# One raw weight tile fewer, one pair of split weight tiles more, in a two-block transformer kernel on one core

## The chip, the core and the metric

One NeuronCore of a Trainium2 chip runs the whole program. The metric is device microseconds (us) of one execution; three executions of the kernel before were timed, and a fourth was profiled.

## The reference, cut to what matters

A sequence of 512 tokens of width 1024 goes through two blocks. The first has two layers, each with three kinds of attention (MLA, differential, chunked) and a gated feed-forward part with a short convolution; the second has a forgetting attention, a state-space part and a mixture of 32 experts. Nearly all of its arithmetic is products with weight matrices:

```python
proj = rms_norm(x, attn_norm[l]) @ w_in[l]
...
x = x + jnp.concatenate([o_mla, o_diff, o_ch], axis=-1) @ w_out[l]
x = x + conv_ffn(rms_norm(x, ffn_norm[l]), w_ffn_in[l], ffn_conv_w[l], ffn_conv_b[l], w_ffn_out[l])
...
z = h @ w_in[l]
mixed = (jax.nn.sigmoid(g_attn) * (y_attn @ w_proj_attn[l])
         + jax.nn.sigmoid(g_ssm) * (y_ssm @ w_proj_ssm[l]))
```

## The kernel before, in words

Each product is computed in three TensorE passes over parts in a reduced format (fp32r): a weight tile `w` is split into `wh` (its rounded value) and `wl` (the rest), the input is split in the same way, and `mm3` (L300 to L304) adds hi by hi, hi by lo and lo by hi. So a weight tile goes through three places:

- `weights` (L306) takes a raw tile `w` of up to 128 x 1024 f32 (4 KB a partition) from pool `wfp` and has SyncE (SP) issue its load from HBM (L311);
- `split` (L291) has ScalarE (ACT) write `wh` (L294) and VectorE (DVE) write `wl` (L295), in a pair of 4 KB tiles from pool `wsp`;
- `proj` (L317) has TensorE (PE) multiply from the pair, 128 columns at a time (L302 to L304).

Before, `wfp` has three raw tiles and `wsp` two pairs. A pair is free again when PE has done its last multiplication from it; a raw tile is free when DVE has written its `wl`. The tiles of the attention inputs (`wp`, `wu`), of the output projections (`wo1` with 640 columns, `wo2` with 768), of the feed-forward parts (`wfi`, `wfo`), and of the second block's `wz`, `wglu`, `wps`, `wpa` (the last three with 512 columns) and `wo` all pass through these two pools. The experts' weights do not: they have pools of their own (`raw`, `mh`, `ml`, L1953 and L1956).

The order of the instructions is set by a planner of the tile framework when the program is built: it plays the program through with estimated durations and gives each engine, at each moment, the ready instruction of highest priority (the order of the program text, with lifts by `prior` for the softmax, L574, and the normalization helpers). An instruction whose tile has no free buffer is not ready. On the chip, each engine, and SP's queue too, then runs that fixed order, waiting on semaphores. From the last step of the second block's output projection on (the experts), the order is that of the program text (L1625).

`newton` (L343) computes a reciprocal square root on DVE in a dozen tiny instructions; its temporaries `nyi` and `na` had six buffers of 32 bytes each (the default of pool `smp`).

The stages, by time in the profile: the first layer's attention to about 305 us, its feed-forward part to 668; the second layer's attention to 958, its feed-forward part to 1320; the second block's mixer to about 1730 and its experts to the end.

Of the kernel before, what the change touches and what calls it, by code (L numbers as in the profile page):

```python
# [57 lines left out]
NRAW = (6, 2, 0, 2)  # L58
# [174 lines left out]
    return a  # L233


BUFS = {"vf": 1, "xs": 2, "sqa": 1, "PT": 6, "E": 4, "B": 2, "V": 2, "u": 5, "lp": 1, "sm": 8, "rs": 8, "ss": 8, "od": 1, "ofd": 2, "xh": 2, "xl": 2, "ye": 3, "raw0": NRAW[0], "raw1": NRAW[1], "raw2": NRAW[2], "raw3": NRAW[3], "mh": 5, "ml": 4, "mh2": 2, "ml2": 2, "ind": 1, "xr": 4, "ud": 4, "fd": 1, "xrd": 1, "stab": 1, "sl": 7, "ix": 7, "yb": 1, "ld": 1, "Bd": 1, "hld": 16, "vd": 8, "gad": 1, "ya": 4, "gs": 8, "ga": 3, "wr": 1, "rsel": 1, "wm": 2, "wr2": 2}


def prior(offset):
# [9 lines left out]
class K:  # L249
# [6 lines left out]
    def T(self, pool, shape, dt, tag):  # L256
        self.n += 1
        return pool.tile(shape, dt, tag=tag, name=f"{tag}_{self.n}", bufs=BUFS.get(tag))

# [930 lines left out]
    def wpart(self, tag):  # L1190

        n = self.parts[tag]
        self.parts[tag] += 1
        return self.T(self.mw2, [128, 1024], F32R, tag + "2") if n % (2 + BUFS[tag]) < 2 else self.T(self.mw, [128, 1024], F32R, tag)

# [838 lines left out]
```

## Time and profile before

| | |
|---|---|
| three timed runs | 2059.34, 2064.02, 2066.14 us; median 2064.02 |
| the profiled execution's own time | 2062.34 us |
| its span, first to last instruction | 2060.6 us |
| mean granted TensorE clock | 0.986 of full speed |
| PE, DVE, ACT busy | 97%, 72%, 53% of the span |
| DMA | 343.7 MB moved, 167 GB/s in the mean |

A wait in the profile is idle time of an engine just before an instruction, put down to what released it. "Busy" of PE counts modelled ends of pipelined multiplications, so it is not a measure of speed by itself: a 128x512 multiplication is shown as some 0.39 us long, though the next one starts some 0.23 us after it. PEld is the loading of the stationary operand, which overlaps PE.

### The profile page before, as it was taken

The page shows a single profiled execution, that of the slowest core. Times are in us where ns is not written, and L with a number is a line of the kernel's source. Part 1 is how long each engine was busy: PE and PEld are TensorE (multiplying, and loading weights), DVE is VectorE, ACT ScalarE, POOL GpSimd, SP SyncE. Part 2 cuts the span into 40 slices and gives each one's busy share as a digit, 9 for nine tenths or more (in the row PEclk, how much of TensorE's full clock was granted, in tenths as well). Part 3 has the DMA queues.
Part 4 walks back from the last instruction along what each step waited for, and adds up shares of the span by engine and source line. Part 5 has one row for each costly group of instructions (what it writes and reads, how often), then busy time and mean ns, then how long its engine had stood idle before and what let it go on. Part 6 is the DMA issues. An engine that isn't in the chain of part 4 may idle for free.

```text
span 2060.6 us, 28191 instructions
## 1 busy us (share of the span) xinstructions
PE 1990.3 (97%) x9836; PEld 1603.3 (78%) x9836; DVE 1478.9 (72%) x2763; ACT 1086.7 (53%) x1760; POOL 64.6 (3%) x132
## 2 busy tenths in 40 slices
PE   7998999999999999989999999999999998999997
PEld 6776778888888878767888888788887876778885
DVE  6787887777633577877777744688756576899996
ACT  5475644444423366644444433334358445788886
POOL 0000000000000000000000000000000000111111
PEclk9998999999999999999999999999999999999999
DMA  5565552323344345634323234344346383899994
GB/s 162 153 196 179 179 166 93 98 97 101 100 123 138 124 125 172 182 127 153 103 92 102 93 113 130 119 157 132 118 152 191 123 282 95 323 333 404 393 405 145
DMA packets 133874, 343.74 MB, mean 167 GB/s; under 512 B 29050, under 2 KB 42618, under 8 KB 121058
## 3 DMA queue, kind: packets, MB, share of 16 engines
q1 hardware_dynamic: 128946, 329.08, 47.4%
q0 software_dynamic: 4640, 12.73, 2.5%
q8 instruction: 79, 1.29, 0.3%
q14 instruction: 65, 0.53, 0.1%
q10 hardware_dynamic: 144, 0.10, 0.0%
HBM read 293.18 MB, written 46.96 MB: 165 GB/s over the span
## 4 chain that ended last, share of the span: by engine, by line
PE 82%; DVE 9%; DMA 3%; ACT 3%; issue 2%; SPq 1%; POOL 0%; DVEq 0%; POOLq 0%; ACTq 0%
PE acc L302 21%; PE acc L303 21%; PE acc L304 21%; PE t L536 2%; DVE ml L1956 2%; PE t L608 2%; PE t L362 1%; PE s L304 1%; PE s L302 1%; PE s L303 1%; DVE wl L295 1%; PE o L548 1%; PE s L850 1%; PE o L549 1%; ACT wh L294 1%
## 5 line engine op out<-in xcount | busy, mean ns | idle before, releaser
L302 PE MATMUL acc<-hb,wh 128*128 128x512 f32 x1392 | 550.5, 396 | 17.4 <-ACT hb L297 11.4
L304 PE MATMUL acc<-hb,wl 128*128 128x512 f32 x1392 | 548.3, 394 | 2.9 <-DVE wl L295 2.8
L303 PE MATMUL acc<-hb,wh 128*128 128x512 f32 x1392 | 547.7, 394 | 0.9 <-DVE hb L295 0.7
L294 ACT ACTIVATE wh<-w 128x1024 fp32r<-128x1024 f32 (+3 forms) x263 | 257.1, 977 | 513.4 <-PE acc L303 371.3
L295 DVE TENSOR_TENSOR wl<-w,wh 128x1024 fp32r<-128x1024 f32 (+3 forms) x263 | 294.9, 1122 | 148.4 <-ACT wh L294 147.8
L302 PEld LDWEIGHTS acc<-hb,wh 128*128 128x128 f32 x1392 | 263.0, 189 | 73.3 <-ACT hb L297 11.4
L304 PEld LDWEIGHTS acc<-hb,wl 128*128 128x128 f32 x1392 | 262.3, 189 | 57.4 <-DVE wl L295 5.4
L303 PEld LDWEIGHTS acc<-hb,wh 128*128 128x128 f32 x1392 | 262.5, 189 | 54.2 <-DVE hb L298 1.4
L1956 DVE TENSOR_TENSOR ml<-raw,mh 128x1024 fp32r<-128x1024 f32 x196 | 231.5, 1224 | 5.9 <-ACT mh L1953 5.1
L1953 ACT ACTIVATE mh<-raw 128x1024 fp32r<-128x1024 f32 x196 | 196.9, 1054 | 8.2 <-DMA raw<-in_we 4.3
L304 PE MATMUL acc<-hid,wl 128*128 128x512 f32 x320 | 126.4, 395 | 0.0
L302 PE MATMUL acc<-hid,wh 128*128 128x512 f32 x320 | 126.4, 395 | 0.0
L303 PE MATMUL acc<-hid,wh 128*128 128x512 f32 x320 | 126.3, 395 | 0.0
L302 PE MATMUL acc<-mh,xh 128*128 128x512 f32 x264 | 108.0, 409 | 0.0
L303 PE MATMUL acc<-ml,xh 128*128 128x512 f32 x264 | 104.6, 396 | 0.0
L304 PE MATMUL acc<-mh,xl 128*128 128x512 f32 x264 | 104.6, 396 | 0.0
L941 DVE TENSOR_TENSOR raw<-acc,R 128x512 f32<-128x512 f32 x88 | 60.6, 688 | 60.7 <-PE acc L304 60.2
L592 ACT ACTIVATE E<-E,mx 128x512 f32<-128x512 f32 (+3 forms) x160 | 88.7, 555 | 27.5 <-DVE mx L590 26.4
L295 DVE TENSOR_TENSOR PT<-t,PT 128x512 fp32r<-128x512 f32 (+1 forms) x120 | 69.2, 597 | 19.1 <-ACT PT L294 18.3
L945 ACT ACTIVATE cv<-raw,sp 128x512 f32<-128x512 f32 x88 | 71.8, 816 | 18.1 <-DVE raw L941 18.1
L536 PE MATMUL t<-cst,E 128*128 128x128 f32 x400 | 74.0, 289 | 5.3 <-DVE E L858 2.7
L294 ACT ACTIVATE PT<-t 128x512 fp32r<-128x512 f32 (+1 forms) x120 | 59.9, 526 | 33.7 <-PE t L536 23.1
(545 smaller groups left out, 3271.8 us busy)
## 6 DMA issues: line engine op xcount, KB each, us to landing
raw<-in_we SPq DMA_DIRECT2D x99, 1024.0 KB, 17.8
w<-in_wfi SPq DMA_DIRECT2D x88, 512.0 KB, 3.4
w<-in_wp SPq DMA_DIRECT2D x34, 512.0 KB, 4.0
w<-in_wfo SPq DMA_DIRECT2D x32, 512.0 KB, 3.6
w<-in_wz SPq DMA_DIRECT2D x32, 512.0 KB, 3.8
hld<-tf SPq DMA_DIRECT2D x56, 256.0 KB, 2.3
qk<-hld SPq DMA_DIRECT2D x96, 128.0 KB, 3.7
qk<-hld SPq DMA_DIRECT2D x192, 64.0 KB, 1.9
```

The lines of the kernel that those rows point to most:

```text
L294: nc.scalar.activation(hi, src, AF.Copy)
L295: nc.vector.tensor_tensor(lo, src, hi.bitcast(F32), op=OP.subtract)
L302: mm(out, lh[0], rh[0], start=start, stop=False)
L303: mm(out, lh[0], rh[1], start=False, stop=False)
L304: self.last_mm = mm(out, lh[1], rh[0], start=False, stop=stop).ins
L536: nc.tensor.transpose(bank[:, c:c + 128], E[:, QOFF[qt] + 128 * kt:QOFF[qt] + 128 * kt + 128], self.c("ident"))
L592: nc.scalar.activation(e, e, AF.Exp, bias=mx, scale=-1.0, accum_out=sm[:, qt:qt + 1])
L608: self.nc.tensor.matmul(pt[64 * h:64 * h + 64, 128 * t:128 * t + 128], f[:, t, h:h + 1].to_broadcast([128, 64]), self.c("ident"), start=Tr ...
L941: nc.vector.tensor_tensor(raw[:, 2:], acc, R, op=OP.mult)
L945: nc.scalar.activation(t, raw[:, 2:], AF.Identity, bias=sp[:, cb:cb + 1], scale=sp[:, cw + 2:cw + 3])
L1953: nc.scalar.activation(hi, w, AF.Copy)
L1956: nc.vector.tensor_tensor(lo, w, hi.bitcast(F32), op=OP.subtract)
```

## The change

Only the table of buffer counts changes. The pools' defaults (L274, L275: three for `w`, two for `wh` and `wl`; L273: six for `na` and `nyi`) give way to entries of their own:

```diff
-BUFS = {"vf": 1, "xs": 2, ...
+BUFS = {"w": 2, "wh": 3, "wl": 3, "na": 3, "nyi": 3, "vf": 1, "xs": 2, ...
```

Per partition, one 4 KB raw tile goes and two 4 KB parts come, and the six buffers of 32 bytes that go make up the rest of the room: everything that is laid out behind `wsp` moves up by 3904 bytes. No instruction is added or removed in the program text.

## Rows read from the trace of the kernel before

**Rows 1.** The page, part 1: busy us (share of the span) xinstructions.
```profile
PE 1990.3 (97%) x9836; PEld 1603.3 (78%) x9836; DVE 1478.9 (72%) x2763; ACT 1086.7 (53%) x1760; POOL 64.6 (3%) x132
```
**Rows 2.** Busy time by stretch: us, busy of each engine (xinstructions), PE clock, DMA.
```profile
200.00:310.00 110.00, 101.62 (x522) 79.56 (x523) 87.74 (x226) 57.75 (x127) 0.17 (x3) 0.94 0.54 176
310.00:490.00 180.00, 180.00 (x796) 149.03 (x795) 129.26 (x166) 80.89 (x101) 3.31 (x33) 1.00 0.29 97
...
860.00:960.00 100.00, 88.51 (x461) 67.40 (x460) 79.70 (x212) 51.84 (x116) 0.16 (x3) 0.95 0.49 154
...
1840.00:1950.00 110.00, 110.00 (x487) 88.33 (x486) 107.34 (x129) 95.92 (x121) 12.12 (x7) 1.00 0.99 378
...
1645.00:1670.00 25.00, 25.00 (x109) 20.04 (x108) 23.01 (x36) 11.80 (x20) 0.00 (x0) 1.00 0.79 275
```
**Rows 3.** Waits of PE, whole run: us in total, times, longest us.
```profile
PE s L850 <- DVE mx L590: 5.7, 13, 1.1
...
PE acc L304 <- DVE wl L295: 2.8, 3, 1.8
PE t L536 <- DVE E L858: 2.7, 4, 1.4
...
PE t L608 <- DVE rs L868: 1.8, 4, 1.2
...
PE acc L302 <- ACT wh L294: 1.3, 1, 1.3
```
**Rows 4.** Waits of ACT, whole run, same columns.
```profile
ACT wh L294 <- PE acc L303: 371.3, 126, 8.6
```
**Rows 5.** ACT in the first feed-forward part, in order of time: start, us, instruction, wait.
```profile
336.44 1.06 ACT L294 ACTIVATE wh<-w 128x1024 fp32r<-128x1024 f32 x1 [2.81 <-PE acc L303]
```
**Rows 6.** SP's queue in the second layer's attention, in order of time.
```profile
881.16 0.43 SPq L311 DMA_DIRECT2D w<-in_wo  x1
```
**Rows 7.** The page, part 6: DMA issues, KB each, median us to landing.
```profile
w<-in_wo SPq DMA_DIRECT2D x16, 320.0 KB, 3.2
...
w<-in_wpa SPq DMA_DIRECT2D x8, 256.0 KB, 3.4
```
**Rows 8.** ACT in the same stretch, in order of time.
```profile
890.64 0.63 ACT L294 ACTIVATE hb<-u 128x512 fp32r<-128x512 f32 x1 [3.20 <-DVE u L869]
891.17 0.72 ACT L294 ACTIVATE wh<-w 128x640 fp32r<-128x640 f32 x1
```
**Rows 9.** PE in the same stretch, in order of time.
```profile
888.73 1.09 PE L608 MATMUL t<-cst,rs 128*64 128x128 f32 x16 [1.21 <-DVE rs L868]
...
891.95 0.50 PE L302 MATMUL acc<-hb,wh 128*128 128x512 f32 x1 [1.26 <-ACT wh L294]
...
893.38 0.50 PE L304 MATMUL acc<-hb,wl 128*128 128x512 f32 x1 [0.70 <-DVE wl L295]
...
904.82 0.80 PE L304 MATMUL acc<-hb,wl 128*128 128x512 f32 x1 [1.77 <-DVE wl L295]
```
**Rows 10.** DVE in the same stretch, in order of time.
```profile
903.20 0.69 DVE L590 CUSTOM_DVE_ANT_0 E<-s,B 128x512 f32<-128x512 f32 x1 [0.30 <-PE s L850]
...
903.95 0.82 DVE L295 TENSOR_TENSOR wl<-w,wh 128x640 fp32r<-128x640 f32 x1
```
**Rows 11.** Loads of line 311 between 1640 and 1730 us: issue to landing.
```profile
DMA to landing us min/median/max: 2.7/5.0/7.1
```
**Rows 12.** Groups between 1640 and 1672 us by shape: count, busy us, mean ns, idle before.
```profile
L295 DVE TENSOR_TENSOR wl<-w,wh 128x512 fp32r<-128x512 f32 x9 | 6.1, 683 | 0.0
L294 ACT ACTIVATE wh<-w 128x512 fp32r<-128x512 f32 x8 | 5.0, 628 | 7.0 <-PE acc L303 6.9
```
**Rows 13.** Line 339 (PE) and line 926 (DVE) in each layer: ns min/median/max, first to last start.
```profile
L339 PE MATMUL s<-hb,wh x7: 387/389/482, 35.8 to 40.6; 128*128 128x512 f32 x7
...
L926 DVE TENSOR_TENSOR hb<-acc,hb x8: 677/684/692, 285.7 to 301.5; 128x512 f32<-128x512 f32 x8
...
L339 PE MATMUL s<-hb,wh x7: 387/389/482, 687.3 to 692.1; 128*128 128x512 f32 x7
...
L926 DVE TENSOR_TENSOR hb<-acc,hb x8: 679/684/692, 935.7 to 951.5; 128x512 f32<-128x512 f32 x8
```

More of the change, by code (lines that the diff above doesn't have):

```diff
@@ L233, in _host @@
     return a
-BUFS = {"vf": 1, "xs": 2, "sqa": 1, "PT": 6, "E": 4, "B": 2, "V": 2, "u": 5, "lp": 1, "sm": 8, "rs": 8, "ss": 8, "od": 1, "ofd": 2, "xh": 2, "xl": 2, "ye": 3, "raw0": NRAW[0], "raw1": NRAW[1], "raw2": NRAW[2], "raw3": NRAW[3], "mh": 5, "ml": 4, "mh2": 2, "ml2": 2, "ind": 1, "xr": 4, "ud": 4, "fd": 1, "xrd": 1, "stab": 1, "sl": 7, "ix": 7, "yb": 1, "ld": 1, "Bd": 1, "hld": 16, "vd": 8, "gad": 1, "ya": 4, "gs": 8, "ga": 3, "wr": 1, "rsel": 1, "wm": 2, "wr2": 2}
+BUFS = {"w": 2, "wh": 3, "wl": 3, "na": 3, "nyi": 3, "vf": 1, "xs": 2, "sqa": 1, "PT": 6, "E": 4, "B": 2, "V": 2, "u": 5, "lp": 1, "sm": 8, "rs": 8, "ss": 8, "od": 1, "ofd": 2, "xh": 2, "xl": 2, "ye": 3, "raw0": NRAW[0], "raw1": NRAW[1], "raw2": NRAW[2], "raw3": NRAW[3], "mh": 5, "ml": 4, "mh2": 2, "ml2": 2, "ind": 1, "xr": 4, "ud": 4, "fd": 1, "xrd": 1, "stab": 1, "sl": 7, "ix": 7, "yb": 1, "ld": 1, "Bd": 1, "hld": 16, "vd": 8, "gad": 1, "ya": 4, "gs": 8, "ga": 3, "wr": 1, "rsel": 1, "wm": 2, "wr2": 2}
 def prior(offset):
```

## The prediction, made blind

> **What bounds the kernel.** I read the busy times first. PE is busy for 1990.3 of 2060.6 us [rows 1], so all that any change of buffers can win lies in what is left, about 70 us, and in the stretches where PE's clock is not fully granted. The table by stretch says where that is. In the feed-forward part PE is busy for 180.00 of 180.00 us at a full clock; there a multiplication starts every 180/796 = 0.226 us, and a tile of 1024 columns (24 of them) lasts 5.4 us. Among the experts PE is busy for 110.00 of 110.00, with DVE at 107.34 and the DMA engines at 0.99. Only the ends of the two attention stages have room: 8.4 us of idle PE in 110 at a clock of 0.94, and 11.5 in 100 at 0.95 [rows 2]. So next I asked what PE waits for. Weight parts come low in the list: 2.8 us in 3 waits for `wl`, 1.3 us in one for `wh`. The softmax and normalization chain costs more: 5.7 (`mx`), 2.7 (`E`), 1.8 (`rs`) [rows 3].
>
> ACT's own list looks quite different: it stood idle for 371.3 us, 126 times, until PE gave a pair back [rows 4]. The reader should not take this for the loss. In the feed-forward part ACT waits 2.81 us for a pair, splits in 1.06 us [rows 5], and DVE follows; the tile that PE is working on lasts 5.4 us, so PE never notices.
>
> **The change, part by part.**
>
> *The third pair in the saturated stretches.* A split can now start one tile earlier. In the feed-forward parts and wherever PE is already at its full rate this moves ACT and DVE work, and gains nothing: PE covers it. The experts use other pools and an order written out by hand. Cost and gain 0 in both.
>
> *The third pair where PE waits for parts.* The list gives 4.1 us at most (2.8 + 1.3) [rows 3]. I looked at the largest. One tile of the output projection is issued at 881.16 [rows 6]; with the median landing of its kind, 3.2 us [rows 7], it is there at about 884.4. Its `wh` is written only at 891.17, behind `hb`, which had kept ACT idle for 3.20 us [rows 8]. Its two users on PE then wait 1.26 and 0.70 us [rows 9]. The pairs before it were in use till shortly before, so the planner may well have held the split back for want of a pair; with a third it could stand right after the landing, ready by about 884.4 + 0.72 + 0.82 = 886 (durations of [rows 8, 10]). I count these 2.0 us as won. The other large wait, 1.77 us at 904.82 [rows 9], is of another kind: `wl` stands in DVE's queue behind a softmax step [rows 10]. A pair doesn't change that; I count nothing. Bounds: 0 to 4.1, taken 2.0.
>
> *More filler.* While the softmax chain runs, PE can only be kept busy by projections whose weights are split. The wait of 1.21 us for `rs` at 888.73 [rows 9] would have found the tile above ready. The three waits on the chain sum to 10.2 us [rows 3]. Bounds: 0 (nothing else to multiply) to 10.2; I take 3, the share that this one example suggests (PE has other work for most of them, or needs inputs that the chain itself makes).
>
> *The clock.* Full speed is 2.4 GHz, and the other level is 1.2. In the two stretches the grant is 0.94 and 0.95, so 6% of 110 us and 5% of 100, together 11.6 us, are lost at most [rows 2]. The idle moments that I expect to vanish are a third or less of those there. Bounds 0 to 11.6; taken 1.
>
> *One raw tile fewer.* From a pair's freeing to the next load the chain is the same as before: what was a raw tile waiting is now a pair waiting, five tiles altogether either way. But a load can only be issued once one of two raw tiles, not three, has been split. For tiles of 1024 columns that is harmless: two of them last 10.9 us, against a load of 7.1 at the longest [rows 11], 1.06 for `wh` [rows 5] and twice 0.68 for `wl` [rows 12], 9.5 together. The `wpa` tiles are short. There PE runs at 109 multiplications in 25 us [rows 2], 0.229 us each; a tile has 12, so 2.75 us. A raw tile's round is its load, 3.4 us over the run [rows 7] but 5.0 in the median and up to 7.1 here [rows 11], while the experts' weights and the gates are on the same DMA engines (share 0.79 [rows 2]), plus 0.63 and 0.68 for the split [rows 12]. With two in flight: (5.0 + 1.3)/2 = 3.15 us a tile, 0.4 more than PE needs, over 8 tiles 3.2 us, less the 2.75 us that the third pair holds in stock: +0.5. With 3.4 it is 2.35 a tile and costs nothing; with 7.1 it is 4.2 a tile, 11.6 - 2.75 = +9. I take +0.5, because the median is of this very stretch.
>
> By the Trainium skill (SBUF — State Buffer, "The DMA setup-cost knee") a transfer takes about 2 us whatever its size, and its bytes at 436 GB/s: 2.6 us for such a tile, an estimate by which this term would be 0. The trace disagrees here: 5.0 in the median; the measurement decides.
>
> SP's queue is in order, so a weight load that waits for its raw tile also holds what is queued behind it (gate tiles, expert weights, `qk` loads). The planner places it when it believes the tile free, so the wait is only its error; I count it in the term above.
>
> *Smaller `na` and `nyi`.* Each is written and read by DVE within a few of its own instructions, in order; three cover three interleaved calls. 0.
>
> *Everything moved up by 3904 bytes.* Pools that reuse the space later wait for other tiles than before. None of the rows shows such a wait on PE's side; 0, bounds -1 and +1.
>
> *A new order.* Since the planner works from buffer availability, all engines' orders before the experts will differ. How much luck lies in an order? The two layers do the same work from line 339 to line 926 in two different orders: 301.5 - 40.6 = 260.9 us and 951.5 - 692.1 = 259.4 us [rows 13], and the first also builds the distance tables. So about 1.5 us a stage; 0 taken, bounds -3 and +3 for the three stages.
>
> Sum: -2.0 - 3 - 1 + 0.5 = -5.5 us, against the profiled execution's own 2062.3 us: 2056.8. The median of the runs shown lies 1.7 above that execution, so I forecast **2058.5 us** for the median.
>
> **The rivals.**
>
> *Filler pays in full.* If the planner always has a split tile for PE in both attention stages, most of 4.1 + 10.2 goes, and some of the 11.6 of clock with it: say -14, 2050 us. For it: the idle lies exactly where projections and softmax are mixed, and ACT's 371.3 us show that pairs are what splits wait for. Against: PE's waits on parts are few.
>
> *Pairs were never the limit.* The late splits are late because ACT and DVE are busy with, or queued behind, the softmax [rows 8, 10]; then nothing changes: 2064. For it: 4.1 us of waits only. The Trainium skill (Perfetto Trace Analysis, "Optimization Strategy") says that too few buffers show as the same gap repeating on the engine that should be saturated. The trace has no such row: PE has no gap at all in the feed-forward part, where most tiles are.
>
> *Two raw tiles starve PE: slower.* The place is the run of short tiles (`wglu`, `wps`, `wpa`) between 1530 and 1670 us; it decides once load plus split exceed two tiles' multiplication, 5.5 us. At 7.1 us a load it costs +9 at `wpa`; with the gains mostly absent, 2064 + 8 = 2072. For it: 5.0 in the median there. Against: the planner can issue early, and the third pair is a stock.
>
> **How the numbers follow.** Chances: the forecast 0.42, filler in full 0.28, nothing 0.16, starved 0.14. About 0.3%, 6.2 us, is what a measurement of this kernel can tell from no change, so "same" reaches from 2057.8 to 2070.2. My forecast lies near its lower edge: of its 0.42 I give 0.12 to faster and 0.02 to slower. Faster: 0.28 + 0.12 = 0.40; slower 0.14 + 0.02 = 0.16; same 0.28 + 0.16 = 0.44. The forecast's own range is 2054 to 2065; with rivals, for 8 in 10, 2046 to 2072: the low end is filler in full with a little clock more, the high end the starved case.
>
> **What would show it.** Right: `wh` of the feed-forward part still waits for PE, but a tile earlier; waits of PE on `wl` and `wh` fall below 2 us; idle PE in the last 100 us of each attention stage shrinks by 2 to 4 us, with a grant above 0.95; the feed-forward and expert stages take as long as before, to 1 us. Wrong: waits of ACT for `w` loads appear between 1640 and 1700 us and PE idles behind them (starved); or the attention stages shrink by over 10 us in all (filler); or the stage lengths change where no pair is in question, which would make the new order the cause.

## The result, and the profile after

The changed kernel takes 2076.64 us (median of 8 runs, 2071.24 to 2082.97), the kernel before 2063.57 us in the runs beside it (8 runs, 2057.31 to 2066.14): a ratio of 1.0069, with a 95% interval of 1.0056 to 1.0083. It is slower by about 13 us, 4.6 us above the upper end of the range.

The page of the changed kernel, part 1, which answers to [rows 1]:

```profile
PE 1999.0 (96%) x9836; PEld 1610.5 (78%) x9836; DVE 1476.1 (71%) x2763; ACT 1086.1 (52%) x1759; POOL 66.2 (3%) x132
```

The span grew by 12.8 us, from 2060.6 to 2073.4. The same 9836 multiplications keep PE busy for 8.7 us longer than in [rows 1], and 4.1 us are added idle time. The work has not grown. The mean granted clock of the two profiled executions fell from 0.986 to 0.981, which over such a span is some 10 us of full-speed time (an estimate), enough for the 8.7 us to be multiplications at the lower clock; busy time counts modelled ends, so the split is not exact.

Busy time by stretch of the changed kernel, which answers to [rows 2] (the last row is shifted by 10 us, since the stage before it ends later):

```profile
200.00:310.00 110.00, 98.49 (x497) 76.42 (x498) 85.76 (x216) 58.87 (x129) 0.17 (x3) 0.92 0.52 175
310.00:490.00 180.00, 180.00 (x803) 149.06 (x803) 129.16 (x175) 79.54 (x100) 3.21 (x32) 1.00 0.28 97
860.00:960.00 100.00, 89.39 (x454) 68.11 (x454) 80.06 (x205) 52.46 (x118) 0.16 (x3) 0.93 0.52 172
1840.00:1950.00 110.00, 109.62 (x484) 87.62 (x483) 107.38 (x134) 94.38 (x120) 13.41 (x6) 1.00 0.97 374
1655.00:1680.00 25.00, 24.32 (x104) 18.98 (x102) 20.75 (x33) 9.47 (x18) 0.00 (x0) 1.00 0.80 277
```

The feed-forward part and the experts are as saturated as before (the 0.38 us of idle time in the row of the experts lie in its first 10 us; from 1850 to 1960 us PE is busy for 110.00 of 110.00). The end of layer 0's attention, from 200 to 310 us, has lost: 98.49 us busy in place of 101.62, at a clock of 0.92 in place of 0.94.

Waits of PE in the changed kernel, which answer to [rows 3], behind one line of the kernel before that those rows leave out:

```profile
PE t L565 <- DMA vf<-vd: 4.0, 1, 4.0
```

```profile
PE t L565 <- DMA vf<-vd: 7.4, 2, 5.1
PE acc L302 <- ACT wh L294: 6.4, 5, 2.9
PE s L850 <- DVE mx L590: 4.3, 10, 1.0
PE acc L304 <- DVE wl L295: 3.8, 4, 1.8
PE t L536 <- DVE E L858: 3.2, 5, 1.8
```

The waits on weight parts were to fall below 2 us. They rose from 4.1 us to 10.2 (6.4 + 3.8). The wait for `vf`, a tile that is also loaded by SyncE's queue, rose from 4.0 to 7.4. The three waits of the softmax chain (`mx`, `E`, `rs`) did not rise: 8.4 us together (4.3 + 3.2 + 0.9) in place of 10.2. ACT's own list, which answers to [rows 4], and one split of the feed-forward part, which answers to [rows 5]:

```profile
ACT wh L294 <- PE acc L303: 390.5, 128, 11.1
```

```profile
342.63 1.06 ACT L294 ACTIVATE wh<-w 128x1024 fp32r<-128x1024 f32 x1 [2.77 <-PE acc L303]
```

ACT still waits for PE to give back a pair, as foreseen, and a pair more makes that wait longer, not shorter.

Where the stages end, which answers to [rows 13] (line 339 opens and line 926 closes the attention of a layer):

```profile
L339 PE MATMUL s<-hb,wh x7: 387/397/475, 35.2 to 39.0; 128*128 128x512 f32 x7
...
L926 DVE TENSOR_TENSOR hb<-acc,hb x8: 676/680/692, 291.5 to 307.7; 128x512 f32<-128x512 f32 x8
...
L339 PE MATMUL s<-hb,wh x7: 387/397/481, 693.6 to 698.3; 128*128 128x512 f32 x7
...
L926 DVE TENSOR_TENSOR hb<-acc,hb x8: 677/682/692, 938.5 to 954.7; 128x512 f32<-128x512 f32 x8
```

Layer 0's attention takes 307.7 - 39.0 = 268.7 us, 7.8 more than before; layer 1's takes 954.7 - 698.3 = 256.4, 3.0 less. From one line 926 to the next line 339 nothing changed: 390.6 us in both (698.3 - 307.7, and 692.1 - 301.5). So the loss has a place to look at first: the attention of layer 0. It isn't the only one. By the end of layer 1's attention 3.2 us of it are left (954.7 against 951.5), and 9.6 of the 12.8 us are lost behind that. The last additions of the eight `wpa` tiles at the end of the mixer (line 1115), before and in the changed kernel:

```profile
L1115 DVE TENSOR_TENSOR ga<-ga,gs x8: 684/684/692, 1652.2 to 1673.3; 128x512 f32<-128x512 f32 x8
```

```profile
L1115 DVE TENSOR_TENSOR ga<-ga,gs x8: 683/685/693, 1661.4 to 1683.4; 128x512 f32<-128x512 f32 x8
```

The changed kernel loses 6.9 us between the two places (10.1 late here, 3.2 late there) and 2.7 behind them. The attention of layer 0 is followed in detail below; the mixer is only timed.

**What is late there.** SyncE's queue in the kernel before, in order of time (start, us, instruction, count):

```profile
134.75 0.33 SPq L311 DMA_DIRECT2D w<-in_wp  x1
...
159.16 7.86 SPq L835 DMA_DIRECT2D qk<-hld  x17
```

The same stretch of the changed kernel:

```profile
159.98 7.26 SPq L835 DMA_DIRECT2D qk<-hld  x16
...
172.32 0.45 SPq L311 DMA_DIRECT2D w<-in_wp  x1
```

It is the load of one and the same weight tile, the 13th of its kind in line 311 in both kernels. Before, a third raw tile came free at 134.72, when VectorE had split the tile three before it, and the load went out at 134.75, ahead of SyncE's runs of small transfers (0.46 us of SyncE's time each, 7.86/17). With two raw tiles it must wait until VectorE has split the tile two before it. In the attention stage VectorE does that late, here from 154.61 to 155.83; by then SyncE is in its runs, and the load stands behind them until 172.32. On PE of the changed kernel:

```profile
180.46 0.50 PE L302 MATMUL acc<-hb,wh 128*128 128x512 f32 x1 [0.71 <-ACT wh L294]
...
182.32 0.50 PE L304 MATMUL acc<-hb,wl 128*128 128x512 f32 x1 [1.12 <-DVE wl L295]
```

That is 1.8 us of waits at this tile, and the multiplications behind it follow late. The load itself had landed 4.0 us after its issue, at 176.3; the split came at 179.36, in the place that ACT's order gave it, against 167.58 before. So on the chip it is the order, written for a late load, that holds the tile, and not the landing. The place lies ahead of the stretch from 200 us on in which the prediction looked for idle time.

A second place lies 70 us on. One row of the table by stretch, of the kernel before and then of the changed one:

```profile
240.00:260.00 20.00, 17.02 (x81) 12.52 (x82) 16.04 (x51) 14.19 (x41) 0.00 (x0) 0.83 0.47 155
```

```profile
240.00:260.00 20.00, 16.45 (x71) 11.76 (x70) 14.74 (x50) 10.95 (x29) 0.00 (x0) 0.74 0.50 161
```

In these 20 us PE did 71 multiplications in place of 81: the softmax chain ran with few projections between its steps, and the clock was granted at 0.74 in place of 0.83. The kernel before has this slump too, some us earlier; it is longer in the changed kernel, by 1.8 us of full-speed time (an estimate: 20 us times the difference of the two grants). How it begins in the changed kernel:

```profile
246.00:250.00 4.00, 2.22 (x8) 1.15 (x7) 3.58 (x14) 3.20 (x12) 0.00 (x0) 0.91 0.84 255
250.00:258.00 8.00, 6.39 (x20) 4.30 (x20) 5.93 (x16) 4.57 (x12) 0.00 (x0) 0.50 0.46 168
```

PE was busy for 2.22 of 4 us, and the next 8 us were granted at 0.50, which is 1.2 GHz in place of 2.4. The Trainium skill (TensorE: Matmul & The Clock Gate, "HAM oscillation — how this bites in real kernels") says that a kernel whose multiplications wait for the next slice of an operand to be loaded begins slice after slice at the lower clock. The trace agrees in this, that the lower clock (0.50) follows a stretch in which PE stood waiting; here the waits were for softmax steps and not for a load.

### The profile page after: what moved, and what is told of

The parts are those of the page before. It is cut to its first block, busy times and chain, and to the rows that moved or that the text cites. A ratio compares the mean times of both kernels' runs of the same rounds, so it can differ in the third digit from the quotient of the medians.

```text
span 2073.4 us, 28225 instructions
## 1 busy us (share of the span) xinstructions
PE 1999.0 (96%) x9836; PEld 1610.5 (78%) x9836; DVE 1476.1 (71%) x2763; ACT 1086.1 (52%) x1759; POOL 66.2 (3%) x132
## 4 chain that ended last, share of the span: by engine, by line
PE 81%; DVE 8%; DMA 3%; ACT 3%; issue 3%; SPq 1%; POOL 0%; DVEq 0%; POOLq 0%; ACTq 0%
PE acc L302 21%; PE acc L303 21%; PE acc L304 21%; PE t L536 2%; DVE ml L1956 1%; PE t L362 1%; PE s L304 1%; PE s L302 1%; PE s L303 1%; PE t L608 1%; DVE wl L295 1%; DMA w<-in_wo 1%; PE s L850 1%; ACT wh L294 1%; PE o L548 1%
## 5 line engine op out<-in xcount | busy, mean ns | idle before, releaser
L302 PE MATMUL acc<-hb,wh 128*128 128x512 f32 x1392 | 552.1, 397 | 21.7 <-ACT hb L297 10.9
L302 PEld LDWEIGHTS acc<-hb,wh 128*128 128x128 f32 x1392 | 264.1, 190 | 78.8 <-ACT hb L297 10.9
L592 ACT ACTIVATE E<-E,mx 128x128 f32<-128x128 f32 (+3 forms) x160 | 88.6, 555 | 24.6 <-DVE mx L590 23.8
```

Of the source, the lines that this page charges most:

```text
L302: mm(out, lh[0], rh[0], start=start, stop=False)
L592: nc.scalar.activation(e, e, AF.Exp, bias=mx, scale=-1.0, accum_out=sm[:, qt:qt + 1])
```

## The experiments

Three theories stood at the start. **Raw depth**: two raw tiles make loads late, as in the rows above. **Third pair**: the earlier splits push other work of ACT and DVE aside. **Order**: no buffer costs anything by itself, but the planner writes another order for every set of buffers, and this one is worse. To tell order from buffers, some kernels are held to an order that was taken from another one, up to the experts, by a dependency between each instruction and the next of its engine:

```diff
+        for a, b in zip(names, names[1:]):
+            self.tc.add_manual_dep(here[b], a, mybir.DependencyInfo(mybir.DependencyClass.NoSync, mybir.DependencyReason.DATA), reason="plan")
```

All ratios are to the kernel before on the same chip, with 95% intervals.

**One part at a time.** w2_alone has two raw tiles and nothing else of the change:

```diff
-BUFS = {"vf": 1,
+BUFS = {"w": 2, "vf": 1,
...
```

> Only the raw tiles change: two in place of three, two pairs of parts as before. Theory 'raw depth' (with two raw tiles a weight's load waits for VectorE's late split of the tile two before it, so weights come late in the attention stages; the third pair has no part in it): all of the loss is here, 2074 to 2078 us, ratio 1.005 to 1.008, and the end of the second projection of layer 0 comes 5 to 8 us late. Theory 'third pair' (the earlier splits of a third pair push other work of ScalarE and VectorE behind them): no loss, 2062 to 2066 us. Theory 'order' (neither buffer costs anything by itself; the planner writes another order for every set of buffers, and this one is worse): in between or anywhere from -5 to +13 us, decided not by the buffers but by the order that comes with them.

Measured: 2076.87 us, 1.0070 [1.0049, 1.0091]. That is the whole loss of the change.

pair3_alone keeps three raw tiles and adds a third `wh` (the room comes from `na` and `nyi`):

```diff
-BUFS = {"vf": 1,
+BUFS = {"wh": 3, "na": 3, "nyi": 3, "vf": 1,
...
```

> Three raw tiles as before, a third tile for the high parts alone (a third tile for the low parts leaves the order of every engine as it is). Theory 'third pair': 2072 to 2078 us. Theory 'raw depth': no loss, 2061 to 2065 us. Theory 'order': from -5 to +13 us with whatever order comes.

Measured: 2058.16 us, 0.9971 [0.9954, 0.9988]: a gain. The theory of the third pair falls, as far as its high part goes. Waits of PE in w2_alone, against [rows 3]:

```profile
PE s L850 <- DVE mx L590: 8.0, 16, 1.6
PE t L565 <- DMA vf<-vd: 6.8, 2, 3.4
PE acc L302 <- ACT wh L294: 5.3, 5, 2.4
```

The waits for `wh` (1.3 us before), for `vf` (4.0) and for `mx` (5.7) have grown; `E` and `rs` have fallen, so that the softmax chain as a whole stands at 10.6 us against 10.2. The second place is there too. In w2_alone the stretch from 240 to 260 us, SyncE's queue, and ACT:

```profile
240.00:260.00 20.00, 14.15 (x61) 9.42 (x59) 14.85 (x53) 12.82 (x39) 0.00 (x0) 0.74 0.37 110
```

```profile
233.96 10.17 SPq L835 DMA_DIRECT2D qk<-hld  x22
...
244.64 0.43 SPq L311 DMA_DIRECT2D w<-in_wo  x1
```

```profile
257.96 0.72 ACT L592 ACTIVATE E<-E,mx 128x512 f32<-128x512 f32 x1
...
258.93 1.37 ACT L294 ACTIVATE wh<-w 128x640 fp32r<-128x640 f32 x2
```

and in the kernel before, SyncE and then ACT:

```profile
232.39 8.78 SPq L835 DMA_DIRECT2D qk<-hld  x19
...
241.69 0.43 SPq L311 DMA_DIRECT2D w<-in_wo  x1
```

```profile
248.08 0.72 ACT L294 ACTIVATE wh<-w 128x640 fp32r<-128x640 f32 x1
```

The load goes out 3 us later (244.64 against 241.69), but its split comes 10.9 us later (258.93 against 248.08), because in ACT's order it now stands behind two more rounds of exponentials. PE did 61 multiplications in this stretch in place of 81. In the changed kernel itself the split stands behind two rounds, as before, and comes at 252.36.

By stage, w2_alone is 4.9 us late at the end of layer 0's attention (306.4 against 301.5 in line 926), 3.5 at the end of layer 1's (955.0 against 951.5), and 12.1 at the last `wpa` tile (1685.4 against 1673.3). So most of its loss, too, comes behind the layers, and 3.1 us of it at the `wpa` tiles themselves, which take 24.2 us from first to last in place of 21.1:

```profile
L1115 DVE TENSOR_TENSOR ga<-ga,gs x8: 683/686/693, 1661.2 to 1685.4; 128x512 f32<-128x512 f32 x8
```

**Whole orders exchanged, some engines left free.** changed_bufs_old_order and old_bufs_new_tensor_order hold some engines to the other kernel's order and leave the rest to the planner.

> The changed kernel's buffers (two raw, three pairs), but TensorE, ScalarE, VectorE and GpSimd are held to the order of the kernel before, up to the experts; SyncE's DMA issues are left to the planner, since the old order of loads cannot be kept with two raw tiles. Theory 'order': 2061 to 2066 us, ratio 0.998 to 1.002. Theory 'raw depth': the loads still wait for the splits, 2070 to 2078 us. Theory 'third pair': about as before, 2062 to 2066, since the splits stand where they stood.

Measured: 2094.75 us, 1.0155 [1.0131, 1.0180].

> The buffers of the kernel before (three raw, two pairs), but TensorE is held to the order of the changed kernel, up to the experts; the other engines are left to the planner. Theory 'order': 2072 to 2077 us, ratio 1.004 to 1.007. Theory 'raw depth': 2062 to 2067 us, since with a third raw tile the weights are there in time whatever the order.

Measured: 2103.07 us, 1.0189 [1.0166, 1.0213]. Both are slower than either kernel, and outside of every expectation. A likely reason is that engines whose order was made for another arrangement fit badly with those that the planner arranges anew; no run shows it. The two tell nothing about the question.

**The order for two raw tiles, with three raw tiles.** Here nothing is left free: all five engines stand in the order of w2_alone, and the third raw tile is given back.

> The buffers of the kernel before (three raw tiles, two pairs), with all five engines held, up to the experts, to the order that the planner wrote for two raw tiles. If the loss of w2_alone is the wait on the chip for a raw tile, the third tile takes it away: 2062 to 2067 us. If it is in the order (the places of the loads in SyncE's queue, or the order of the compute engines), nothing changes: 2073 to 2078 us, ratio 1.005 to 1.008.

Measured: 2072.57 us, 1.0045 [1.0032, 1.0058]. Neither expectation is quite met: about two thirds of w2_alone's 0.70% stay though the tile is there. Whether the last third really goes is at the edge of the two intervals, which were measured on two chips. Line 926 of layer 0 (line 1072 in this kernel) shows that layer 0's loss stays in full:

```profile
L1072 DVE TENSOR_TENSOR hb<-acc,hb x8: 681/684/693, 292.2 to 308.0; 128x512 f32<-128x512 f32 x8
```

With SyncE left to the planner:

> As raw3_order_of_raw2, but SyncE is left to the planner, which with three raw tiles can set the loads of weights ahead of SyncE's runs of small transfers again; TensorE, ScalarE, VectorE and GpSimd keep the order for two raw tiles. If the places of the loads in SyncE's queue carry the loss: 2062 to 2068 us. If the order of the compute engines carries it: 2072 to 2078 us.

Measured: 2078.05 us, 1.0075 [1.0062, 1.0088]. Read with the two kernels above, this is again an order that is half one plan and half another, and it doesn't show that the compute engines carry the loss.

**The gain of the third `wh` in the old order.**

> Three raw tiles and a third tile for high parts, with all five engines held to the order of the kernel before, up to the experts. If the gain of pair3_alone (2058.2 us, ratio 0.997) is the new order that the third tile allows: 2062 to 2065 us, as before. If it is a wait on the chip that the third tile removes within the old order: 2057 to 2060 us.

Measured: 2060.38 us, 0.9975 [0.9963, 0.9987], against 0.9971 with its own order. So the gain is the buffer's and not the order's: it is there with every instruction in its old place.

**More raw tiles.** raw4_alone has four, in the same room:

```diff
-BUFS = {"vf": 1,
+BUFS = {"w": 4, "na": 3, "nyi": 3, "vf": 1,
...
```

> Four raw tiles, two pairs. Theory 'raw depth' (loads have to run ahead of SyncE's runs of small transfers and of VectorE's late splits): no loss and perhaps a further gain, 2056 to 2064 us. Theory 'order' as a mere lottery of plans: 200 of TensorE's 6851 instructions of the layers and the mixer stand elsewhere, anything from -5 to +13 us.

Measured: 2066.21 us, 1.0016 [1.0005, 1.0027]. More depth gives nothing; with the order that came with it the kernel loses 0.16%. So the planner doesn't turn a raw tile more into time. Whether it is the order that costs these few us was not tested.

**Loads on a queue of their own.**

```diff
...
-            nc.sync.dma_start(w, src)
+            (nc.gpsimd if self.inlayers else nc.sync).dma_start(w, src)
...
```

`inlayers` is true while the two layers are written. The planner writes a new order for these kernels; nothing is held.

> The kernel before (three raw tiles, two pairs), with the loads of the weights of the two layers (200 of them, not those of the mixer) issued by GpSimd, which has almost nothing else to do, in place of SyncE, where they stand between runs of up to 27 small transfers of 0.5 us each. It is the control of raw2_loads_own_queue. Theory 'queue' (weights come late because their loads stand behind those runs): no loss, perhaps a gain, 2054 to 2064 us. Theory 'raw depth' as VectorE's late splits alone: as before, 2060 to 2067.

Measured: 2086.34 us, 1.0115 [1.0100, 1.0130].

> Two raw tiles, two pairs, and the layers' loads on GpSimd's queue. Theory 'queue' (the third raw tile is what lets a load be issued ahead of SyncE's runs; on a queue of their own the loads need no such lead): at the end of layer 1 within 2 us of raw3_loads_own_queue, where w2_alone was 3.5 us later than before (4.9 at the end of layer 0); the mixer, whose loads stay on SyncE, may still lose up to 8 us. Theory 'raw depth' as VectorE's late splits alone: 4 to 8 us later at the end of layer 0, since the splits release the raw tiles no sooner, and 8 to 14 us in all.

Measured: 2087.54 us, 1.0116 [1.0100, 1.0131]. The difference that the raw tile made is 1.2 us in all, in place of 13.4. The last tile of layer 1 (line 979, here 983) even ends earlier with two; raw3_loads_own_queue first, then raw2_loads_own_queue:

```profile
L983 DVE TENSOR_TENSOR xs<-acc,xs x16: 691/692/692, 570.2 to 1339.8; 128x512 f32<-128x512 f32 x16
```

```profile
L983 DVE TENSOR_TENSOR xs<-acc,xs x16: 691/692/692, 565.3 to 1333.9; 128x512 f32<-128x512 f32 x16
```

So in the layers, where the loads no longer pass through SyncE's queue, two raw tiles cost nothing, as theory 'queue' says. Behind the layers, where they still pass through it, the profile of raw2_loads_own_queue loses the 5.9 us again and 5.4 more (spans of 2089.3 and 2083.9 us); part of that is its execution, which is 3.6 us slower than its median. That leaves the raw tile worth something in the mixer. The evidence is weakened by the level of both kernels: they are some 23 us slower than before, which theory 'queue' had not expected, and a kernel that waits elsewhere may hide what a raw tile is worth. Waits of PE in raw2_loads_own_queue:

```profile
PE acc L304 <- DVE hb L890: 12.1, 5, 3.0
...
PE t L612 <- DVE rs L872: 9.6, 4, 2.8
```

PE now waits 12.1 us for VectorE's line 890, which empties the accumulators of the output projections, and 9.6 for `rs`, where before `rs` took 1.8 [rows 3]. Why both kernels are slower was not settled. PE may use up its projections early, so that little is left to multiply at the end of the attention; the new order may be a worse one; and the queue itself may be: in raw3_loads_own_queue GpSimd is busy for 173.1 us in place of 64.6 [rows 1], and the `in_wo` loads land after 4.2 us in the median in place of 3.2 [rows 7]. The Trainium skill (Trainium Kernel Development and Optimization, "Key Constraints") says that issuing from several queues saves only the time of the sequencer that issues. No run here measures that time by itself; saving it on SyncE didn't shorten this kernel.

> The changed kernel (two raw tiles, three pairs) with its layers' loads on GpSimd's queue. Theory 'queue': the third pair's gain (5 us in pair3_alone, all of it in the layers) shows again: 2 to 7 us below raw2_loads_own_queue. Theory 'raw depth': no better than the changed kernel, 2072 to 2080 us.

Measured: 2086.48 us, 1.0107 [1.0092, 1.0122], the same as without the third pair within the intervals. The pair's gain doesn't show beside two raw tiles here either.

**Both buffers at three.** The room comes from other tiles:

```diff
-NHB = 22
+NHB = 20
...
-BUFS = {"vf": 1,
+BUFS = {"wh": 3, "wl": 3, "na": 3, "nyi": 3, "vf": 1,
...
-"u": 5,
+"u": 4,
...
```

> Three raw tiles and three pairs, both parts; the room is taken from two of 22 tiles of layer inputs (hb) and one of five of attention outputs (u). If the third pair pays wherever the raw tiles stay three: 2055 to 2061 us, as pair3_alone or a little less (the third low part lets VectorE's splits run ahead too). If the two hb tiles were needed: 2062 to 2070.

Measured: 2065.63 us, 1.0000 [0.9985, 1.0014]. The gain of pair3_alone is not there; the cost of the tiles given up was not measured apart.

**Which part of the order.** Four kernels more, each composed of two orders at one instruction, all with three raw tiles. The executions of one such kernel spread over some 10 us, and each stage time is read from a single one.

> The buffers of the kernel before (three raw tiles, two pairs). All five engines are held up to the experts: to the order for two raw tiles (that of raw3_order_of_raw2) up to the last matmul of the second projection tile of layer 0 (243 us in both traces), and from there on to the order of the kernel before. If layer 0's loss is made in the stretch from 243 to 260 us, where the order for two raw tiles splits the next weight only behind two sets of exponentials: layer 0's second projection ends within 3 us of before (301.5), 2061 to 2067 us in all. If it is made earlier: 305 to 308 there.

Measured: 2068.22 us, 1.0022 [1.0007, 1.0037]. Layer 0's line 926:

```profile
L1072 DVE TENSOR_TENSOR hb<-acc,hb x8: 681/684/692, 289.3 to 305.0; 128x512 f32<-128x512 f32 x8
```

> The other half: the order of the kernel before up to that same matmul, then the order for two raw tiles. If the stretch from 243 to 260 us makes layer 0's loss: the second projection of layer 0 ends 4 to 7 us late (305 to 309), 2069 to 2074 us in all. If it is made earlier: 300 to 303 there, and 2063 to 2068 in all (the mixer's part alone).

Measured: 2072.82 us, 1.0045 [1.0031, 1.0059]:

```profile
L1073 DVE TENSOR_TENSOR hb<-acc,hb x8: 681/684/692, 286.5 to 302.2; 128x512 f32<-128x512 f32 x8
```

The either-or was not settled. The first part of the order alone makes layer 0 3.5 us late (305.0 against 301.5), and the second part alone 0.7; together it was 6.5. But the first profile is of the third slowest of its kernel's 12 executions (2073.34 us), and the second of the fastest of 12 (2067.55). Both halves lose in the medians, by 4.5 and 9.1 us; whether they sum to more than the 9.2 of raw3_order_of_raw2 is within the intervals.

> Three raw tiles, the order for two raw tiles through both layers, the order of the kernel before in the mixer. raw3_order_of_raw2 lost 6.5 us in layer 0, gave 2.9 back in layer 1 and lost 5 from there to the last wpa tile. If the stages are independent: 2065 to 2069 us, with the layers 3 to 4 us late and the mixer as before.

Measured: 2069.49 us, 1.0028 [1.0013, 1.0043]. Layer 0's line 926, and the last `wpa` tile of the mixer (line 1115, here 1264):

```profile
L1075 DVE TENSOR_TENSOR hb<-acc,hb x8: 679/682/692, 293.6 to 309.3; 128x512 f32<-128x512 f32 x8
...
L1264 DVE TENSOR_TENSOR ga<-ga,gs x8: 684/684/693, 1657.1 to 1677.0; 128x512 f32<-128x512 f32 x8
```

Layer 0 is late again (7.8 us), and with the old order in the mixer the last `wpa` tile is 3.7 late, where raw3_order_of_raw2 is 8.5. So the layers carry some 6 us of the order's 9, and what is left for the mixer is 3 us, which the intervals do not separate from nothing.

> Three raw tiles and a third tile for high parts; the order of pair3_alone through both layers and that of the kernel before in the mixer. pair3_alone gained 7 us in the layers and gave 2 back in the mixer's first part, so if the stages are independent: 2054 to 2058 us, the fastest here; if the mixer's loss was no matter of order: 2058 to 2060, as pair3_alone.

Measured: 2056.31 us, 0.9961 [0.9947, 0.9976]. Layer 0's line 926, for the two kernels with a third `wh`, pair3_alone first:

```profile
L926 DVE TENSOR_TENSOR hb<-acc,hb x8: 683/688/692, 281.5 to 297.1; 128x512 f32<-128x512 f32 x8
```

```profile
L1072 DVE TENSOR_TENSOR hb<-acc,hb x8: 679/684/692, 283.7 to 299.3; 128x512 f32<-128x512 f32 x8
```

It is the fastest of all kernels here and beats both of the pair, by 0.4% and by about 1%; from pair3_alone its interval does not separate it. One profile of the same order in a stage differs by about 2 us from the next (281.5 and 283.7 above), so single stage times of less than that are not to be read.

## Why the prediction was wrong

**The step that failed is "One raw tile fewer".** It was priced at +0.5 us; by itself it costs 13.4 (w2_alone). The step treated the raw tiles as a matter of rate, a load plus a split against the multiplications of two tiles, and asked that only where tiles are short, at `wpa`. At that place it was nearly right: w2_alone takes 3.1 us longer over the eight tiles (24.2 in place of 21.1), against the 3.2 that the step had without the third pair's stock, and the changed kernel 0.9 (22.0), against +0.5. Just behind them the sign of the starved case shows too, PE standing behind the load of the first `wo` tile:

```profile
1682.24 0.50 PE L302 MATMUL acc<-hb,wh 128*128 128x512 f32 x1 [2.92 <-ACT wh L294]
```

But in the attention stages a raw tile isn't held for 1.3 us after landing. It is held until VectorE comes to its low part, behind the softmax, and its next load stands in SyncE's queue behind runs of small transfers (16 and 22 in the rows above). There the third tile bought not rate but the chance to send the load ahead of such a run: 37.6 us earlier in SyncE's rows above (134.75 against 172.32). The sentence that the planner places a load when it believes the tile free, "so the wait is only its error", is where this was dismissed: the load of those rows did not wait at the head of the queue for its tile, it stood far back, and two thirds of the cost stay when the tile is given back in that order. Whether SyncE's places or those of the compute engines carry these two thirds is not shown. The step before it, that only the ends of the two attention stages have room, failed with it: the first late tile lies at 180 us, ahead of the stretch that was read, and 9.6 of the 12.8 us come behind the second attention.

**"A new order", 0 with bounds of 3, was mis-sized.** The order for two raw tiles costs 9.2 us with the third tile given back (raw3_order_of_raw2), three times the bound; the changed kernel's own order, which has the third pair besides, was not measured in this way. The bound came from two layers that do the same work in two orders [rows 13], but both of those orders were written for the same buffers. They say what luck does, not what an order must give up when a buffer is taken from it. When the program is built with the smaller `na` and `nyi` alone, or with a third `wl` beside them, every engine's order stays as it was, so the planner's order doesn't change with every buffer.

**The third pair.** In the saturated stretches it gains nothing, as said: 180.00 us of 180.00 in both. Elsewhere the steps foresaw 6 us (2.0 + 3 + 1), and pair3_alone gained 5.3, so the size was right, for a third `wh` beside three raw tiles. The split into terms was not shown: the waits on parts did not fall in it, as these rows of pair3_alone show against [rows 3], its clock stayed at 0.985 (0.986 before), and the three waits on the chain fell by 1.2 us only (9.0 in place of 10.2).

```profile
PE s L850 <- DVE mx L590: 5.4, 12, 1.1
PE acc L304 <- DVE wl L295: 3.1, 4, 1.8
...
PE t L536 <- DVE E L858: 2.5, 3, 1.4
...
PE acc L302 <- ACT wh L294: 1.3, 1, 1.3
...
PE t L608 <- DVE rs L868: 1.1, 3, 0.6
```

In pair3_old_order, which gained as well, the chain's waits rose to 11.4 (6.6 + 3.0 + 1.8). So a right size here is luck as far as the terms go, and which wait the third `wh` shortens stays open. In the change itself nothing of this gain is left: w2_alone, without it, takes as long (2076.87 against 2076.64). Layer 1's 3.0 us are no trace of it: raw3_order_of_raw2, which has no third pair, takes 2.9 us less there too (6.5 late at the end of layer 0's attention, 3.6 at the end of layer 1's). Why it vanishes beside two raw tiles was not settled; that a pair can be filled no earlier than its load comes would explain it, and is only argued.

**`na`, `nyi` and the addresses**, at 0: nothing found speaks against it. raw4_alone and pair3_alone have the smaller `na` and `nyi` and the shifted pools, and the latter is faster.

**The rivals.** "Pairs were never the limit" falls with pair3_alone, which gained although PE has no repeating gap. "Filler pays in full" was no case of this change. "Two raw tiles starve PE" named the right buffer and the right sign, and its 2072 was the nearest figure, with a chance of 0.14; its place, the short tiles up to `wpa`, carries only a part of the loss, and its condition, load plus split above 5.5 us at short tiles, leaves out what the order costs in layer 0.

**What stays open.** What loses 6.9 us in the changed kernel between layer 1's attention and the last `wpa` tile, and how much of that is of the order and how much of the single execution; why four raw tiles lose; and which of the order's places in layer 0 costs how much, since the two halves of it were timed in executions that are too far apart.

## What to carry to other kernels

Ask of every buffer that is taken away who gives it back and where its next load stands in the queue that issues it: a spare raw tile in front of an in-order queue can be worth more than the time of one load, since it lets the load go out ahead of a run of other transfers. Where a planner writes the order from the buffers, price a buffer that binds by the order it allows, and try each buffer of an exchange alone; here the half that was the aim gave 0.3% and the half that paid for its room took 0.7%. Keep the better half if there is other room for it.

## What was not expected of the hardware

SyncE needs about 0.46 us to issue one of the small transfers (10.17 us for 22, 7.86 for 17), so a run of them holds the next weight load for longer than that load itself takes to land (3.2 us in the median for `in_wo` [rows 7]).

With the 200 loads of the layers on GpSimd's queue, where they no longer stood behind those runs, the time rose by 23 us; the cause was not found.

Idle time was the smaller part of the loss: of 12.8 us of span 4.1 were idle, and PE was busy for 8.7 us longer with the same multiplications, while its mean clock fell from 0.986 to 0.981.
